# A sink as a 385th column of each head's logits, and inverses taken two heads at a time, in a hybrid encoder layer on one Trainium2 core

## The chip, the core and the metric

The kernel runs on one core of one Trainium2 chip. Five engines work side by side, each through its own list of instructions in a fixed order: TensorE (PE, with its weight loads as a list PEld of their own in the profile), VectorE (DVE), ScalarE (ACT), GpSimd (POOL) and SyncE (SP), which here issues most of the DMAs. An engine waits on a semaphore where its next instruction needs what another has made. The metric is the device time of one execution in microseconds (us); lower is better. Matmuls write to PSUM, everything else lives in SBUF with 128 partitions.

## What is computed

One encoder layer over 4096 tokens of 1024 numbers. Half of the mixing is attention within a window, with eight query heads on two key heads and a learned sink for each head; the other half is a pooling mixer. Both are gated, multiplied by an output matrix, normalised and added to the input.

```python
def banded_attention(q, k, v, rel_bias, sink):
    ...
    s = jnp.einsum('bnqkgd,bnskd->bnkgqs', qb, kw).astype(jnp.float32) * scale
    ...
    s = jnp.where(valid[None, :, None, None], s + bias[None, None], NEG)
    sk = sink.astype(jnp.float32).reshape(1, 1, N_KV_HEADS, Q_PER_KV, 1, 1)
    m = jnp.maximum(jnp.max(s, axis=-1, keepdims=True), sk)
    p = jnp.exp(s - m)
    p = p / (jnp.sum(p, axis=-1, keepdims=True) + jnp.exp(sk - m))
    o = jnp.einsum('bnkgqs,bnskd->bnqkgd', p.astype(v.dtype), vw)
    return o.reshape(B, S, N_Q_HEADS * HEAD_DIM)

def reference(x, pre_norm_g, w_in, rel_bias, attn_sink, pool_w, pool_scale, w_out, post_norm_g):
    ...
        h = rmsnorm(x, pre_norm_g[l])
        proj = jnp.einsum('bsd,de->bse', h, w_in[l])
        q, k, v, g_a, u_p, g_p = jnp.split(proj, splits, axis=-1)
        ...
        a = banded_attention(q, k, v, rel_bias, attn_sink[l]) * jax.nn.silu(g_a)
        p = multiscale_pool(u_p, pool_w[l], pool_scale[l]) * jax.nn.silu(g_p)
        mixed = jnp.einsum('bse,ed->bsd', jnp.concatenate([a, p], axis=-1), w_out[l])
        x = x + rmsnorm(mixed, post_norm_g[l])
    return x
```

A block of 128 queries sees three blocks of keys (its own and both neighbours), which makes 384 logits for each query and head; the first and the last block of the sequence see two, 256 logits. The sink has no key and no value: it only adds one term to the sum of exponentials, and takes part in the maximum.

## The kernel before, in words

The program has two phases. In the first, up to about 488 us, it normalises the input, scales the weights, and makes the gates and the pooling half. There the table of biases for the attention is made as well: `bias_load` fetches it into the tile `ybig` (the name `bias` is a view of it, eight heads by 384 columns, and `gpost` is another view behind it), `bias_head` (L679, on DVE) rescales and masks it head by head, and `bias_scales` makes `nsink`, the negative sinks (L658, DVE, 128x8).

In the second phase the 32 blocks are gone through from the last to the first (b = 31, 30, ... 0). Each block has two visits (half 0 and 1) with four of the eight heads each, so there are 64 visits. One visit, written (b, half), is this chain across the engines:

- `scores` (PE, L1530) puts the products of queries and keys into the two PSUM tiles of `s_bank`, two heads in each.
- `logits` (DVE, L1548), one custom instruction for each head: adds the bias, negates and scales, writes the result to the tile `p_all`, and leaves the smallest value, with the negative sink among the candidates, in `nm` (the negated maximum).
- `exps` (ACT, L1559), one for each head: exponentials in place in `p_all`, and their sum in `den`.
- `sinks` (DVE, L1566, 128x4): `nm` minus `nsink`, into `rd`; `sink_exps` (ACT, L1575, 128x4): its exponential, the sink's term.
- `denominators` (DVE): add the sink's term to `den` (L1579), take the reciprocal (L1580), multiply by a constant (L1581), all 128x4.
- `probs` (ACT, L1595), one for each head: `p_all` times the inverse, as float16, into `pn`. `rests` (DVE, L1603), one for each head: what float16 left out, as a second float16.
- `turn` (SP, L1615): one DMA that transposes `pn` into `pt_all`. Some time later, `values` (PE, L1849 and L1872) multiplies it by the values.

There is one `p_all` and one pair of `s_bank` tiles, and two buffers of `pn`. `logits` and `exps` go through the heads as i = 0 to 3 with `jj, gg = divmod(i, 2)` and `hh = 2 * gg + jj`, so the heads come in the order 0, 2, 1, 3; `probs` and `rests` go 0, 1, 2, 3.

Between the visits PE makes the projections of queries and keys (L1756, L1714, L1493), and the product with the output matrix (L2019) in several parts, for whose operands ACT, DVE and POOL make sums and casts (L1921 to L1963, tiles `y`, `ys`, `yf`, `at`), and whose partial results DVE adds up (L2061, tiles `mo` and `xt`).

The order on each engine is fixed by a plan. Every step is entered with a due time by `due(t, fn, ...)`; the list is sorted by these numbers, and instructions go out in that order whatever the engines do. `visit` sets the time t at which a visit's softmax starts, and `softmax` enters its steps at set distances from t. `settled` moves other steps (casts, sums, additions) away from the places that the softmax steps take, by rules on t alone. The last part of the program has its times written out, with `soft` in the place of `softmax`. So a step's place among its neighbours follows from these distances, and a step that leaves or joins at the same distance leaves the neighbours in place.

Of the kernel before, what the change touches and what calls it, by code (L numbers as in the profile page):

```python
# [8 lines left out]
F32 = mybir.dt.float32  # L9
# [20 lines left out]
QR = 32  # L30
NK = 2 * P + QR

W_BUFS = 6
# [38 lines left out]
def hybrid_layer(ctx: ExitStack, tc, io, out):  # L72
# [28 lines left out]
    wq_a = raw16[:, 4 * D :].rearrange("p (s a j k c) -> p s a j k c", s=4, a=2, j=2, k=HK)  # L101
    yflat = ybig.rearrange("p s d -> p (s d)")
    bias = yflat[:, : NH * 3 * P].rearrange("p (h k) -> p h k", h=NH)
    gpost = yflat[:, NH * 3 * P :]

# [49 lines left out]
    with ExitStack() as actx:  # L155
# [484 lines left out]
        def bias_load():  # L640

            f0 = f_scr[0:1, 0, :]
            for p0 in range(0, P, FR):
                nc.sync.dma_start(
                    bias[p0 : p0 + FR],
                    bass.AP(
                        tensor=f0.tensor, offset=f0.offset + P - 1 - p0,
                        ap=[[NF - 1, FR], [(FR + 1) * NF, NH], [1, 3 * P]],
                    ),
                )  # L650
# [27 lines left out]
        def bias_head(h):  # L678
            nc.vector.scalar_tensor_tensor(  # L679
                out=bias[:, h, :], in0=bias[:, h, :], scalar=invc[:, h : h + 1], in1=row_t["m"],  # L680
                op0=ALU.mult, op1=ALU.add,
            )
# [709 lines left out]
        for h in range(NH):  # L1392
            at_(7, 28.0 + 1.2 * h, bias_head, h)

        for m in range(1, NM):
# [158 lines left out]
    def exps(b, half, i):  # L1554
        nk = len(keys(b)) * P
        jj, gg = divmod(i, 2)
# [16 lines left out]
    def sink_exps(b, half):  # L1573
        es = rd_t[b, half][:, 1]
        nc.scalar.activation(es, es, AF.Exp)  # L1575

    def denominators(b, half):
        den, rd = den_t.pop((b, half)), rd_t[b, half]
        nc.vector.tensor_tensor(out=den, in0=den, in1=rd[:, 1], op=ALU.add)  # L1579
        nc.vector.reciprocal(rd[:, 0], den)  # L1580
        nc.vector.tensor_scalar(  # L1581
            out=rd[:, 0], in0=rd[:, 0], scalar1=P_SCALE, scalar2=None, op0=ALU.mult
        )
# [5 lines left out]
    def probs(b, half, i):  # L1589
        nk = len(keys(b)) * P  # L1590
        if i == 0:
            pn_t[b, half] = pb.tile(
# [24 lines left out]

    starts = []

    def softmax(b, half, t):  # L1620
# [707 lines left out]
    def soft(b, half, tl, te, td, tp, tr, tt):  # L2328

        at_(tl + 2.5, sinks, b, half)  # L2330
        at_(te + 2.6, sink_exps, b, half)
        for i in range(4):
            at_(tl + 0.62 * i, logits, b, half, i)
            at_(te + 0.65 * i, exps, b, half, i)
            at_(tp + 0.55 * i, probs, b, half, i)
            at_(tr + 0.62 * i, rests, b, half, i)
        at_(td, denominators, b, half)
# [189 lines left out]
```

## Time and profile before

| what | value |
|---|---|
| time, median of three runs | 1161.64 us |
| the three runs | 1160.58, 1161.64, 1161.92 us |
| the profiled execution's own time | 1160.95 us |
| its span (first to last instruction) | 1159.2 us |
| TensorE clock granted, mean | 0.998 of full speed |
| ACT busy | 757.9 us |
| POOL busy | 287.1 us |

In what follows, a row of the timeline reads: start in us, duration in us, engine, line of the kernel, operation, out<-in, shape, how many in a run (x), and in brackets how long the engine stood idle before it and what released it. A run of several rows of one kind is drawn together, with the time from the first start to the last end. A row of the groups reads: line, engine, operation, out<-in, shape, count, then the busy time in us and the mean duration of one in ns, then the idle time just before them. A row of windows reads: window, its length, busy us of PE, PEld, DVE, ACT and POOL (with the count of instructions), the granted clock, the share of DMA time and GB/s. A row with "SPq" is a DMA on the queue that SyncE issues, from issue to landing.

### The profile page before, as it was taken

How to read it: one execution, taken by the hardware profiler on the slowest of the kernel's cores; microseconds unless marked ns; L12 is line 12 of the kernel's file. 1: busy time of each engine (PE TensorE's matmuls, PEld its weight loads, DVE VectorE, ACT ScalarE, POOL GpSimd, SP SyncE). 2: the span in 40 equal slices, each digit the busy share in tenths (PEclk: the TensorE clock that was granted, in tenths of full speed). 3: DMA queues.
4: the chain of work that ended last, by engine and by line, in shares of the span. 5: the costliest groups of instructions: out<-in, count | busy, mean ns of one | idle time of the engine just before them, and what ended most of it. 6: DMA issues, size and time to landing. Idle time of an engine off the chain costs nothing.

```text
span 1159.2 us, 29335 instructions
## 1 busy us (share of the span) xinstructions
PE 1123.2 (97%) x11952; PEld 828.6 (71%) x11952; DVE 923.8 (80%) x1910; ACT 757.9 (65%) x1696; POOL 287.1 (25%) x273
## 2 busy tenths in 40 slices
PE   5999999999999999999899999999999999999997
PEld 4548888888888888887576676667666666766643
DVE  5888787788878976957887878878778778778896
ACT  5766666676465535156687767767777777777673
POOL 1000000000000000001364444445354454544322
PEclk9999999999999999999999999999999999999999
DMA  9567898796979856999799999899799899899977
GB/s 257 159 234 265 216 268 286 261 312 221 305 225 284 267 210 165 342 280 254 202 196 219 216 224 199 192 227 201 173 228 221 182 219 222 198 223 211 174 190 215
DMA packets 312630, 264.92 MB, mean 229 GB/s; under 512 B 214528, under 2 KB 275584, under 8 KB 303792
## 3 DMA queue, kind: packets, MB, share of 16 engines
q1 hardware_dynamic: 308464, 248.38, 77.8%
q0 software_dynamic: 4032, 14.68, 7.6%
q8 instruction: 93, 1.52, 0.5%
q14 instruction: 41, 0.34, 0.1%
HBM read 132.97 MB, written 79.21 MB: 183 GB/s over the span
## 4 chain that ended last, share of the span: by engine, by line
PE 61%; DVE 13%; DMA 11%; issue 5%; ACT 4%; SPq 1%; POOL 1%; DVEq 0%; POOLq 0%; ACTq 0%
PE ms L2019 12%; PE aq_p L1756 10%; PE m L2019 9%; PE ch L990 5%; PE s L1530 4%; DMA rs_scr<-ssq 3%; PE kv L1493 3%; PE kv L1714 3%; PE a L940 3%; PE cl L990 3%; DVE ws L855 3%; PE o L1872 3%; DMA xn<-in_x 2%; DVE xt L303 2%; DMA pt_all<-pn 2%
## 5 line engine op out<-in xcount | busy, mean ns | idle before, releaser
L990 PEld LDWEIGHTS <-wa 128*128 128x128 f16 x3360 | 328.8, 98 | 44.4 <-issue 6.6
L990 PE MATMUL ch<-xt,wa 128*128 128x256 f16 x1920 | 212.6, 273 | 2.7 <-ACT cbig L1002 2.6
L1559 ACT ACTIVATE p_all<-p_all,nm 128x384 f32<-128x384 f32 (+1 forms) x256 | 152.4, 596 | 41.5 <-DVE nm L1548 41.5
L1603 DVE SCALAR_TENSOR_TENSOR pn<-p_all,rd,pn 128x384 f16<-128x384 f32 (+1 forms) x256 | 144.4, 623 | 36.9 <-ACT pn L1595 36.2
L2019 PE MATMUL ms<-wo,ys 128*128 128x512 f16 x720 | 165.4, 379 | 3.8 <-DVE xt L2061 1.3
L1595 ACT ACTIVATE pn<-p_all,rd 128x384 f16<-128x384 f32 (+1 forms) x256 | 134.7, 597 | 36.7 <-DVE rd L1581 17.6
L1548 DVE CUSTOM_DVE_ANT_0 p_all<-s,ybig,nsink 128x384 f32<-128x384 f32 (+1 forms) x256 | 155.7, 664 | 1.7 <-PE s L1530 1.7
L2019 PEld LDWEIGHTS <-ys 128*128 128x128 f16 x720 | 68.8, 98 | 85.2 <-issue 4.1
L2019 PE MATMUL m<-wo,y 128*128 128x512 f16 x540 | 124.0, 379 | 1.4 <-DVE mo L2061 1.3
L990 PE MATMUL cl<-xt,wa 128*128 128x256 f16 x960 | 106.9, 273 | 2.5 <-DVE u L1015 1.4
L1925 POOL TENSOR_TENSOR y<-yf,y 128x512 f16<-128x512 f32 x29 | 33.6, 1159 | 268.2 <-DMA wo<-w_scr 158.7
L2019 PEld LDWEIGHTS <-y 128*128 128x128 f16 x540 | 51.6, 98 | 62.4 <-issue 2.8
L1756 PEld LDWEIGHTS <-raw 128*128 128x128 f16 x864 | 83.2, 98 | 17.6 <-issue 5.7
L211 POOL TENSOR_SCALAR ssq<-ssq 128x4 f32<-128x4 f32 (+1 forms) x11 | 4.8, 440 | 346.7 <-ACT jk L202 340.8
L1756 PE MATMUL aq_p<-xt,raw 128*128 128x256 f16 x672 | 77.9, 273 | 0.0
L303 DVE TENSOR_TENSOR xt<-ybig,xt 128x1024 f16<-128x1024 f32 x56 | 67.2, 1218 | 13.1 <-ACT xt L298 13.1
L1925 POOL TENSOR_TENSOR ys<-at,ys 128x512 f16<-128x512 f32 x28 | 33.8, 1206 | 147.1 <-ACT ys L1921 123.5
L1024 ACT ACTIVATE gp<-cbig,cg 128x256 f32<-128x256 f32 x42 | 19.0, 499 | 69.7 <-DVE cbig L1015 66.5
L2056 POOL TENSOR_TENSOR mo<-mo,ybig 128x512 f32<-128x512 f32 x39 | 51.3, 1316 | 41.8 <-ACT jkb L2045 41.6
L1530 PE MATMUL s<-k_all,q 64*32 64x288 f16 (+2 forms) x2856 | 60.1, 284 | 1.5 <-ACT k_all L1481 0.9
L298 ACT CAST xt<-ybig 128x1024 f16<-128x1024 f32 x56 | 57.1, 1040 | 4.0 <-PE cl L990 2.1
L1756 PE MATMUL aq_p<-xt,wq_b 128*128 128x256 f16 x504 | 58.6, 273 | 0.0
(212 smaller groups left out, 1947.5 us busy)
## 6 DMA issues: line engine op xcount, KB each, us to landing
x_scr<-xt SPq DMA_DIRECT2D x16, 1024.0 KB, 4.0
xt<-x_scr SPq DMA_DIRECT2D x16, 1024.0 KB, 5.0
xn<-in_x SPq DMA_DIRECT2D x28, 512.0 KB, 7.2
ybig<-in_xT SPq DMA_DIRECT2D x28, 512.0 KB, 6.9
y_scr<-xt SPq DMA_DIRECT2D x14, 1024.0 KB, 8.6
xt<-y_scr SPq DMA_DIRECT2D x14, 1024.0 KB, 6.2
mo<-in_x POOLq DMA_DIRECT2D x28, 512.0 KB, 7.2
out<-mo SPq DMA_DIRECT2D x28, 512.0 KB, 7.0
```

The source lines that it names most:

```text
L298: nc.scalar.copy(couple(m, c)[:, w, 0], y_view(i))
L303: eng.tensor_tensor(out=o[:, w, 1], in0=y_view(i), in1=o[:, w, 0], op=ALU.subtract)
L990: nc.tensor.matmul(acc[:, c], wa[:, q, wi, slot * HK + k, c * P : (c + 1) * P], x[:, xi, k, :], start=(fresh and n == 0), stop=(n > 3 * 2 ...
L1530: nc.tensor.matmul(s_bank[jj][r0 : r0 + nr, gg, lo:hi], q_t[u, half][a, qi, jj, tl + r0 : tl + r0 + nr], k_all[a, ki, k0 : k0 + hi - lo], ...
L1548: nc.vector.tensor_tensor_reduce(out=p_t[b, half][:, hh, :nk], in0=s_t[b, half][jj][:, gg, :nk], in1=bias[:, h, lo : lo + nk], scale=negc[ ...
L1559: nc.scalar.activation(p[:, hh, :nk], p[:, hh, :nk], AF.Exp, bias=nm_t[b, half][:, hh : hh + 1], scale=-1.0, accum_out=den_t[b, half][:, h ...
L1595: nc.scalar.activation(prob_view(b, half)[:, 0, i], p_t[b, half][:, i, :nk], AF.Copy, scale=rd_t[b, half][:, 0, i : i + 1],)
L1603: nc.vector.scalar_tensor_tensor(out=pn4[:, 1, i], in0=p_t[b, half][:, i, :nk], scalar=rd_t[b, half][:, 0, i : i + 1], in1=pn4[:, 0, i], o ...
L1756: nc.tensor.matmul(acc[:, jj], w[:, wi, jj, k, :], x[:, xi, k, :], start=(first and n == 0), stop=(last and n > 3 * 2 * HK - 3), skip_grou ...
L1925: eng.tensor_tensor(out=y[:, :, 1], in0=f(u), in1=y[:, :, 0], op=ALU.subtract)
L2019: nc.tensor.matmul(z_t[u, tag], y[:, k, yi, :], wo[o][:, wi, k, :], start=(n == 0 and acc is None), stop=(n == 3 * HK - 1), skip_group_che ...
L2056: eng.tensor_tensor(out=mo, in0=mo, in1=gpost[:, cs], op=ALU.mult)
```

## The change

For the 30 blocks that are not at an end of the sequence (`inner(b)`, 60 of the 64 visits) the sink becomes one more column of the logits. A row of the bias is now 386 wide (`BW`), of which 385 (`NC`) are used; column 384 holds the sink times `invc` (made once by `bias_sinks`, a 128x8 multiplication on DVE), and column 384 of the PSUM tiles is set to zero once (`zero_column`, two memsets on DVE of 128x2). `logits` and `exps` run over 385 columns, so that the sum of exponentials has the sink's term in it; `probs`, `rests` and `turn` still take 384. In these visits `sinks`, `sink_exps` and the addition L1579 are gone. The reciprocal and the multiplication are done twice, over two heads each (128x2): by `inverses(b, half, 0)` for heads 0 and 2 at the distance at which `sinks` stood, and by `inverses(b, half, 1)` for heads 1 and 3 at that of `denominators`. `probs` and `rests` take the heads in the order 0, 2, 1, 3. The four visits of the blocks 31 and 0 keep the steps of before. In the written-out last part, `soft` is changed as `softmax` is.

```diff
+NC = 3 * P + 1
+BW = 3 * P + 2
...
-    ybig = const.tile([P, 4, D], F32, name="ybig")
+    yflat = const.tile([P, NH * BW + D], F32, name="ybig")
+    ybig = yflat[:, : 4 * D].rearrange("p (s d) -> p s d", s=4)
...
-    bias = yflat[:, : NH * 3 * P].rearrange("p (h k) -> p h k", h=NH)
-    gpost = yflat[:, NH * 3 * P :]
+    bias = yflat[:, : NH * BW].rearrange("p (h k) -> p h k", h=NH)
+    gpost = yflat[:, NH * BW :]
...
         def bias_head(h):
             nc.vector.scalar_tensor_tensor(
-                out=bias[:, h, :], in0=bias[:, h, :], scalar=invc[:, h : h + 1], in1=row_t["m"],
-                op0=ALU.mult, op1=ALU.add,
+                out=bias[:, h, : 3 * P], in0=bias[:, h, : 3 * P], scalar=invc[:, h : h + 1],
+                in1=row_t["m"], op0=ALU.mult, op1=ALU.add,
+            )
+
+        def bias_sinks():
+
+            def column(t):
+                return t.rearrange("p (h o) -> p h o", o=1)
+
+            nc.vector.tensor_tensor(
+                out=bias[:, :, 3 * P : NC], in0=column(row_t["sk"]), in1=column(invc), op=ALU.mult
+            )
...
+        at_(7, 37.0, bias_sinks)
...
-    p_all = pb1.tile([P, 4, 3 * P], F32, name="p_all")
+    p_all = pb1.tile([P, 4, BW], F32, name="p_all")
...
+    def inner(b):
+        return 0 < b < NB - 1
+
+    def columns(b):
+        return NC if inner(b) else len(keys(b)) * P
+
+    def zero_column():
+        for i in range(2):
+            nc.vector.memset(s_bank[i][:, :, 3 * P : NC], 0.0)
+
+    due(0.0, zero_column)
...
     def logits(b, half, i):
-        kbs = keys(b)
-        nk, lo, j0 = len(kbs) * P, kbs[0] * P, 2 * half
+        nk, lo, j0 = columns(b), keys(b)[0] * P, 2 * half
...
     def exps(b, half, i):
-        nk = len(keys(b)) * P
+        nk = columns(b)
...
+    def inverses(b, half, j):
+        den, rd = den_t[b, half][:, j : 4 : 2], rd_t[b, half][:, 0, j : 4 : 2]
+        nc.vector.reciprocal(rd, den)
+        nc.vector.tensor_scalar(out=rd, in0=rd, scalar1=P_SCALE, scalar2=None, op0=ALU.mult)
+
     def denominators(b, half):
+        if inner(b):
+            return inverses(b, half, 1)
...
     def softmax(b, half, t):
         starts.append(t)
-        due(t + 2.8, sinks, b, half)
-        due(t + 3.25, sink_exps, b, half)
+        if inner(b):
+            due(t + 2.8, inverses, b, half, 0)
+        else:
+            due(t + 2.8, sinks, b, half)
+            due(t + 3.25, sink_exps, b, half)
         for i in range(4):
             due(t + 0.1 + 0.67 * i, logits, b, half, i)
             due(t + 0.8 + 0.8 * i, exps, b, half, i)
-            due(t + 4.5 + 0.6 * i, probs, b, half, i)
-            due(t + 5.1 + 0.62 * i, rests, b, half, i)
+            due(t + 4.5 + 0.6 * i, probs, b, half, ORDER[i])
+            due(t + 5.1 + 0.62 * i, rests, b, half, ORDER[i])
         due(t + 4.3, denominators, b, half)
         due(t + 7.8, turn, b, half)
```

In the program as it is built, the lists of PE, POOL and SP are the same before and after, waits included. ACT's list is 60 rows shorter, by the 60 `sink_exps`. DVE's is 3 rows longer, by the two memsets and the product of `bias_sinks`; in each of the 60 visits four small instructions stand where four stood.

On ACT, the visit (30, 0), the first of the inner ones. A name such as `pn_0_6416` is a tile, its buffer and a running number; "x4" is four instructions of one kind in a row. Before:

```order
L1559 ACTIVATE p_all,den_0_6400<-p_all,nm_0_6399 128x384 x4
L1575 ACTIVATE rd_0_6401<-rd_0_6401 128x4
L1595 ACTIVATE pn_0_6416<-p_all,rd_0_6401 128x384 x4
L1921 CAST y_15_6449<-yf_15_6011 128x4x128
L1481 ACTIVATE q_0_6451<-aq_0_6347 128x512
```

and after the change (the line numbers are those of the changed kernel):

```order
L1582 ACTIVATE p_all,den_0_6403<-p_all,nm_0_6402 128x385 x4
L1625 ACTIVATE pn_0_6418<-p_all,rd_0_6404 128x384 x4
L1955 CAST y_15_6451<-yf_15_6014 128x4x128
L1493 ACTIVATE q_0_6453<-aq_0_6350 128x512
```

The exponentials of the four heads are now followed directly by `probs`.

On DVE, the visit (28, 0), with two steps of other work among its own: `kq` belongs to a projection, `mo` is a partial sum of the output product. Before:

```order
L1566 TENSOR_TENSOR rd_0_6994<-nm_0_6992,nsink 128x4
L1806 SCALAR_TENSOR_TENSOR kq_1_7019<-aq_p_6958,kq_1_6216 128x512
L1579 TENSOR_TENSOR den_0_6993<-den_0_6993,rd_0_6994 128x4
L1580 RECIPROCAL rd_0_6994<-den_0_6993 128x4
L1581 TENSOR_SCALAR rd_0_6994<-rd_0_6994 128x4
L1603 SCALAR_TENSOR_TENSOR pn_0_7065<-p_all,rd_0_6994,pn_0_7065 128x384 x3
```

and after:

```order
L1602 RECIPROCAL rd_0_6993<-den_0_6992 128x2
L1603 TENSOR_SCALAR rd_0_6993<-rd_0_6993 128x2
L1840 SCALAR_TENSOR_TENSOR kq_1_7019<-aq_p_6957,kq_1_6219 128x512
L1602 RECIPROCAL rd_0_6993<-den_0_6992 128x2
L1603 TENSOR_SCALAR rd_0_6993<-rd_0_6993 128x2
L1633 SCALAR_TENSOR_TENSOR pn_0_7063<-p_all,rd_0_6993,pn_0_7063 128x384 x3
```

One reciprocal and one multiplication now stand ahead of the other work, in the place of `sinks`, and one of each behind it, in the place of three instructions.

On DVE, the visit (27, 0), where an addition of the output product (`mo`) stands right behind the step that changes. Before:

```order
L1566 TENSOR_TENSOR rd_0_7293<-nm_0_7291,nsink 128x4
L2061 TENSOR_TENSOR mo_1_7221<-ms_15_7278,mo_1_7221 128x512
L1579 TENSOR_TENSOR den_0_7292<-den_0_7292,rd_0_7293 128x4
L1580 RECIPROCAL rd_0_7293<-den_0_7292 128x4
L1581 TENSOR_SCALAR rd_0_7293<-rd_0_7293 128x4
```

and after:

```order
L1602 RECIPROCAL rd_0_7290<-den_0_7289 128x2
L1603 TENSOR_SCALAR rd_0_7290<-rd_0_7290 128x2
L2095 TENSOR_TENSOR mo_1_7218<-ms_15_7275,mo_1_7218 128x512
L1602 RECIPROCAL rd_0_7290<-den_0_7289 128x2
L1603 TENSOR_SCALAR rd_0_7290<-rd_0_7290 128x2
```

The addition has two instructions ahead of it where it had one.

More of the change, by code (lines that the diff above doesn't have):

```diff
@@ L644, in bias_load @@
                 nc.sync.dma_start(
-                    bias[p0 : p0 + FR],
+                    bias[p0 : p0 + FR, :, : 3 * P],
                     bass.AP(
@@ L2328, in soft @@
     def soft(b, half, tl, te, td, tp, tr, tt):
-        at_(tl + 2.5, sinks, b, half)
-        at_(te + 2.6, sink_exps, b, half)
+        if inner(b):
+            at_(tl + 2.5, inverses, b, half, 0)
+        else:
+            at_(tl + 2.5, sinks, b, half)
+            at_(te + 2.6, sink_exps, b, half)
         for i in range(4):
@@ L2334, in soft @@
             at_(te + 0.65 * i, exps, b, half, i)
-            at_(tp + 0.55 * i, probs, b, half, i)
-            at_(tr + 0.62 * i, rests, b, half, i)
+            at_(tp + 0.55 * i, probs, b, half, ORDER[i])
+            at_(tr + 0.62 * i, rests, b, half, ORDER[i])
         at_(td, denominators, b, half)
```

4 lines of the change are left out of this document (2 added, 2 removed).

## The prediction

> **What bounds the kernel now.** I read the page's first part, then the windows of the second phase, then the timeline of PE for every place where it waits.
>
> ```profile
> PE 1123.2 (97%) x11952; PEld 828.6 (71%) x11952; DVE 923.8 (80%) x1910; ACT 757.9 (65%) x1696; POOL 287.1 (25%) x273
> ...
> 900.00:1000.00 100.00, 100.00 (x1265) 66.71 (x1263) 78.63 (x206) 74.57 (x187) 45.89 (x43) 1.00 0.89 202
> ```
>
> PE is busy for 97% of the span, and in the hundred microseconds from 900 for all of it, at full clock. A softmax that gets shorter there is worth nothing: DVE's 78.63 and ACT's 74.57 lie under PE's work. The change touches nothing on PE, so what it can win is the idle time of PE. Behind 488 us the waits of PE above 0.2 us are these:
>
> ```profile
> 488.16 0.71 PE L1756 MATMUL aq<-xt,raw 128*128 128x256 f16 x5 [0.21 <-DVE u L1015]
> ...
> PE s L1530 <- ACT k_all L1481: 0.9, 2, 0.5
> ...
> 525.28 1.91 PE L1756 MATMUL aq<-xt,raw 128*128 128x256 f16 x16 [1.14 <-DVE q L1484]
> ...
> 554.65 0.60 PE L2019 MATMUL ms<-wo,ys 128*128 128x512 f16 x2 [0.53 <-ACT ys L1921]
> ...
> 555.89 2.33 PE L2019 MATMUL ms<-wo,ys 128*128 128x512 f16 x10 [0.63 <-POOL ys L1925]
> ...
> 573.92 2.75 PE L2019 MATMUL m<-wo,y 128*128 128x512 f16 x12 [1.30 <-DVE mo L2061]
> ...
> 577.12 2.75 PE L2019 MATMUL ms<-wo,ys 128*128 128x512 f16 x12 [0.44 <-DVE mo L2061]
> ...
> 622.98 0.85 PE L1849 MATMUL o<-pt_all,vv 128*64 128x256 f16 x12 [0.90 <-DMA pt_all<-pn]
> ...
> 769.28 1.92 PE L1493 MATMUL kv<-xt,raw 128*128 128x256 f16 x16 [1.13 <-DVE den L1579]
> ...
> 805.90 0.85 PE L1849 MATMUL o<-pt_all,vv 128*64 128x256 f16 x12 [0.35 <-DMA pt_all<-pn]
> ...
> 1115.34 4.92 PE L2019 MATMUL ms<-wo,ys 128*128 128x512 f16 x22 [0.85 <-DVE ys L1925]
> ...
> 1121.22 0.50 PE L1530 MATMUL s<-k_all,q 64*128 64x256 f16 x6 [0.42 <-DVE nm L1548]
> ...
> 1122.02 2.75 PE L2019 MATMUL ms<-wo,ys 128*128 128x512 f16 x12 [0.29 <-DVE xt L2061]
> ...
> 1127.88 2.32 PE L2019 MATMUL ms<-wo,ys 128*128 128x512 f16 x10 [1.03 <-DVE xt L2061]
> ```
>
> They sum to 10.1 us: 9.22 in the thirteen rows with a start, 0.9 in the two waits of the scores for `k_all`. Those two lie in the visits of block 31, which the change leaves alone, and the 0.21 stands ahead of the first visit. At most some 9 us, 0.8% of the time, can be had, in a start-up (525 to 577), three single places, and the last blocks (1115 to 1128).
>
> **The cost of the wider rows.**
>
> ```profile
> L1548 DVE CUSTOM_DVE_ANT_0 p_all<-s,ybig,nsink 128x384 f32<-128x384 f32 x240 | 147.9, 672 | 0.0
> ...
> L855 DVE TENSOR_TENSOR ws<-ws 128x521 f32<-128x521 f32 x16 | 11.2, 703 | 0.6
> ...
> L1548 DVE CUSTOM_DVE_ANT_0 p_all<-s,ybig,nsink 128x256 f32<-128x256 f32 x16 | 7.7, 540 | 1.7 <-PE s L1530 1.7
> ```
>
> A custom instruction of 384 columns takes 672 ns and one of 256 takes 540, so a column costs (672-540)/128 = 1.0 ns, and the 385th 4 ns a visit. That an odd count is dearer no row of the custom instruction can show; the nearest row with an odd count is 521 columns at 703 ns, against 0.69 us for 512 in the row of L1484 below, the same 1 ns a column. I take 0 for both `logits` and `exps`. The other end: 60 ns an instruction, 0.24 us a visit, as much as a quarter of what a visit gains below.
>
> **The three new instructions ahead.**
>
> ```profile
> 464.73 0.62 DVE L679 SCALAR_TENSOR_TENSOR ybig<-ybig,invc,mask 128x384 f32<-128x384 f32 x1 [4.90 <-DMA ybig<-f_scr]
> ...
> 464.73:488.16 23.43, 22.68 (x208) 20.02 (x206) 22.74 (x38) 4.21 (x11) 0.00 (x0) 1.00 0.96 358
> ```
>
> The memsets come on DVE shortly before the 4.90 us that it waits for the bias: covered, 0; without that cover they would cost 0.3, two at the price of the smallest instructions shown below. `bias_sinks` stands behind the wait, in a stretch where DVE is busy for 22.74 of 23.43 us up to the row at 488.16, at which PE waits for DVE. It costs its length there: **+0.2** (0.16 for a small one, a little for the stride of 386); from 0 to 0.5.
>
> **One visit.** The first inner visit, (30, 0):
>
> ```profile
> 519.89 0.60 ACT L1559 ACTIVATE p_all<-p_all,nm 128x384 f32<-128x384 f32 x1
> 520.49 0.19 ACT L1575 ACTIVATE rd<-rd 128x4 f32<-128x4 f32 x1
> ...
> 520.91 0.18 DVE L1580 RECIPROCAL rd<-den 128x4 f32<-128x4 f32 x1
> 521.12 0.17 DVE L1581 TENSOR_SCALAR rd<-rd 128x4 f32<-128x4 f32 x1
> 521.38 2.13 ACT L1595 ACTIVATE pn<-p_all,rd 128x384 f16<-128x384 f32 x4 [0.70 <-ACT rd L1575]
> ...
> 522.02 2.21 DVE L1603 SCALAR_TENSOR_TENSOR pn<-p_all,rd,pn 128x384 f16<-128x384 f32 x4 [0.73 <-ACT pn L1595]
> ...
> 524.54 0.69 DVE L1484 SCALAR_TENSOR_TENSOR q<-aq,q 128x512 f16<-128x512 f32 x1 [0.31 <-ACT q L1481]
> ```
>
> The exponentials end at 520.49; the sink's exponential and three small instructions on DVE follow, and the first of `probs` starts at 521.38. After the change the inverses of heads 0 and 2 are made while the last two exponentials run, so `probs` can start at 520.5: 0.88 us sooner. The second pair needs one reciprocal and one multiplication behind the last exponential, done at about 521.0, and the third of `probs` would come at 520.5 + 2 x 0.53 (2.13 for four) = 521.56, so it waits for nothing. `rests` (0.64 behind), the copy of q on ACT, and the addition at 524.54 move with it. PE's 1.14 at 525.28 falls to about 0.3: **-0.86**, from 0 to -1.14.
>
> Where ACT has other work between the exponentials and `probs`, less is won:
>
> ```profile
> 548.81 0.19 ACT L1575 ACTIVATE rd<-rd 128x4 f32<-128x4 f32 x1
> 548.90 0.57 ACT L2045 ACTIVATE jkb<-m 128x512 bf16<-128x512 f32 x1
> 549.69 2.13 ACT L1595 ACTIVATE pn<-p_all,rd 128x384 f16<-128x384 f32 x4
> ```
>
> Here, in (29, 1), the square `jkb` starts 0.09 sooner and its end, not the inverse, releases `probs`: 549.69 - 548.90 = 0.79 is left from its start to the first of `probs`, of which 0.57 remains, so 0.09 + 0.22 = 0.3. The other visit of block 29 I put at 0.4, also with a filler. DVE's chain to the sums that PE waits for at 554.65 and 555.89 is that much earlier: **-0.73** of the 1.16 there, from 0 to -1.16.
>
> The 1.30 at 573.92 hangs on `mo`, which in DVE's order stands behind the `rests` of both visits of block 28. Each gains 0.6 to 0.8, by the same reckoning, together more than the stall: **-1.30**, from 0.
>
> At 577.12 it goes the other way. In the third order of the section on the change, `mo` has two dependent small instructions ahead of it where it had one that it could follow at once.
>
> ```profile
> 576.30 0.16 DVE L1566 TENSOR_TENSOR rd<-nm,nsink 128x4 f32<-128x4 f32 x1
> 576.38 0.68 DVE L2061 TENSOR_TENSOR mo<-ms,mo 128x512 f32<-128x512 f32 x1
> ```
>
> It started 0.08 after `sinks`; dependent small instructions follow each other at 0.21 (520.91 to 521.12), so two of them take 0.41: **+0.33**, from 0.1 to 0.8.
>
> **The transposes.** PE's 0.90 at 622.98 waits for a transpose:
>
> ```profile
> 596.82 0.63 DVE L1566 TENSOR_TENSOR rd<-nm,nsink 128x4 f32<-128x4 f32 x1
> ...
> 601.53 7.68 SPq L1615 DMA_TRANSPOSE pt_all<-pn  x1
> ```
>
> The transposes come one behind another, this one taking 7.68 us. I let half a microsecond of the visit's gain through: **-0.5**, from 0 to -0.9. The 0.35 at 805.90 is of the same kind: **-0.3**. At 769.28 the addition of `den` is named, but PE's matmul reads the loaded `xt`, not `den`; I leave the 1.13 as it is: 0, from -1.13.
>
> **The end.**
>
> ```profile
> 1095.00:1128.00 33.00, 30.29 (x294) 15.50 (x293) 30.13 (x71) 22.95 (x61) 6.30 (x5) 1.00 0.74 189
> ...
> 1116.46 2.13 ACT L1595 ACTIVATE pn<-p_all,rd 128x384 f16<-128x384 f32 x4 [1.61 <-issue]
> ```
>
> DVE is busy for 30.13 of 33 us and paces PE: waits of 0.85, 0.42, 0.29 and 1.03. Its list has as many small instructions in an inner visit as before; what goes is its own wait for ACT (0.73 ahead of `rests`, as at 522.02), in the two visits of block 1. In the second of these ACT had been free for 1.61 us ahead of 1116.46, so `probs` can be done before DVE comes, and 0.8 is won; of the first I count nothing more, since its gain is met by PE's own pace: **-0.8**, from 0 to -2.6.
>
> **The sum.** +0.2 - 0.86 - 0.73 - 1.30 + 0.33 - 0.5 - 0.3 - 0.8 = -3.96. The profiled execution took 1160.95, so 1156.99; the median of the runs shown is 0.69 above it, and 1157.7 is the time to compare.
>
> **A rule against the change.** The multiplication has moved to a place where POOL is often at work.
>
> ```profile
> 558.36 1.16 POOL L1925 TENSOR_TENSOR ys<-at,ys 128x512 f16<-128x512 f32 x1
> 558.56 0.98 DVE L1581 TENSOR_SCALAR rd<-rd 128x4 f32<-128x4 f32 x1
> ...
> L1566 DVE TENSOR_TENSOR rd<-nm,nsink 128x4 f32<-128x4 f32 x64 | 21.1, 329 | 2.2
> ```
>
> A TENSOR_SCALAR of 0.17 took 0.98 and ended with POOL's instruction, and `sinks`, at 0.16 when alone, took 0.329 on the mean, so its place often meets one. The Trainium skill ("SBUF — State Buffer", "Who interferes with whom") says that the port pair which DVE and GpSimd share is an exclusive lock: whoever issues first has it for the whole instruction, and the other stands still. The row at 558.56 agrees with it; by that rule each of the 60 first multiplications could stand still for a whole POOL instruction. The price goes by the rows: 0.98 - 0.17 = 0.81 a meeting. But two exponentials pass between the first multiplication's place and the end of the visit's exponentials, 1.2 us at the 0.60 of the row at 519.89, and a POOL instruction of 1.16 ends within that. I count nothing.
>
> **The rivals.**
>
> The transposes pin the stream (chance 0.16). If the DMA queue, not the softmax, sets when the transposes ahead of 622.98 land, the 3 us won before it are lost as a longer wait there, and only 805.90 and the end are left: -1.1, so **1160.5**. For it: 7.68 us for one transpose, and DMA 0.89 to 0.96 busy in the two windows above. Against it: a transpose is issued when `rests` end, and these come sooner.
>
> It does little (0.08). DVE issues no fewer small instructions in a visit than before; only their places differ. If the copies and squares on ACT cover the gap in most of the places above, as `jkb` half does, and the multiplications take the rest, it is under 0.5: **1161.3**.
>
> Slower (0.07): the lock above. It decides where POOL's instructions come in pairs, so that the first multiplication outlasts the 1.2 us, and where DVE sets the pace: the two visits each of the start-up's and the end's blocks. At five such places with 0.81 each and nothing won it is +4: **1165.7**. `sinks` stood in the same place under the same lock, which speaks against any loss over before.
>
> More goes (0.09): all the waits that a softmax feeds vanish, 7.44 of the 9.22 without those at 488.16, 577.12 and 769.28; with +0.2 and +0.33 that is -6.9: **1154.7**.
>
> **How the numbers follow.** The forecast has 0.60, from 1155.8 to 1159.3: the bounds of its terms add up to 3.4 us below the sum (without the 1.13 at 769.28) and 5.3 above it, and as the terms don't all err together I give it 1.9 below and 1.6 above. 0.2% of the median is 2.3 us, about what a measurement of this kernel can tell from no change; faster by more than that is 0.60 + 0.09 = 0.69, the same 0.16 + 0.08 = 0.24, slower 0.07. A range to 1161.2 takes in the forecast, most of the pinned case and part of the one that does little; down to 1155.0 it takes a part of the best one; some 2 in 10 are left out.
>
> **What would show it.** In the profile after: `probs` right behind the exponentials at (30, 0), 0.9 sooner against `scores`; DVE's wait for ACT ahead of `rests` (0.73) gone where ACT has a filler; PE's waits at 525, 554, 556 and 574 together under 1 us, the one at 577 near 0.8; the first custom instructions of 385 columns at 0.67 us. A longer wait at 622.98 would show the transposes; `rests` starting as late as before would show a cover that I missed; custom instructions or exponentials clearly above their 0.67 and 0.60 would make the whole forecast wrong, since 240 of each then add to DVE and ACT.

## The result, and the profile after

The changed kernel takes 1161.44 us (median of 20 runs, 1157.72 to 1163.02), the kernel before 1163.71 (median of 20, 1160.17 to 1166.80): a ratio of 0.9977 with a 95% interval of 0.9966 to 0.9988, or 1.4 to 4.0 us less. The forecast was faster by 4.0 us, 1157.7, with a range to 1161.2; the time lies 0.2 us above it. Two things are in this miss. The kernel before took 1161.64 in the three runs that the forecast started from, and 2.1 more in twenty; and of the 4.0 us only 2.3 came by the two medians, or 2.7 by the ratio (1163.71 x 0.0023).

The page's first part, of the profiled execution after the change:

```profile
PE 1123.0 (97%) x11952; PEld 828.7 (72%) x11952; DVE 923.5 (80%) x1913; ACT 748.5 (65%) x1636; POOL 295.4 (25%) x273
```

ACT, without the 60 sink exponentials, is busy for 9.4 us less, and DVE's busy time is what it was. POOL has the same 273 instructions as before, but is busy for 295.4 us instead of 287.1: some of its instructions take longer, and rows further down show one that waits inside. The groups of the changed lines (columns as in the section on the profile before), and behind them that of `rests` in the kernel before:

```profile
L1571 DVE CUSTOM_DVE_ANT_0 p_all<-s,ybig,nsink 128x385 f32<-128x385 f32 x240 | 148.2, 676 | 0.0
...
L1633 DVE SCALAR_TENSOR_TENSOR pn<-p_all,rd,pn 128x384 f16<-128x384 f32 x240 | 145.0, 664 | 18.0 <-ACT pn L1625 17.3
...
L1603 DVE TENSOR_SCALAR rd<-rd 128x2 f32<-128x2 f32 x120 | 31.4, 262 | 4.1
...
L1602 DVE RECIPROCAL rd<-den 128x2 f32<-128x2 f32 x120 | 19.4, 162 | 5.5 <-ACT p_all L1582 5.1
```

```profile
L1603 DVE SCALAR_TENSOR_TENSOR pn<-p_all,rd,pn 128x384 f16<-128x384 f32 x240 | 137.1, 630 | 35.0 <-ACT pn L1595 34.2
```

The 385th column costs 4 ns of 676, its odd number included. What DVE no longer spends waiting for `probs` ahead of the first `rests` (18.0 us now, 35.0 before) it partly spends inside `rests`, 664 ns each instead of 630.

The visit (30, 0) in the timeline, to be set against the one of before:

```profile
522.35 0.60 ACT L1582 ACTIVATE p_all<-p_all,nm 128x385 f32<-128x385 f32 x1
522.35 0.17 DVE L1603 TENSOR_SCALAR rd<-rd 128x2 f32<-128x2 f32 x1
522.95 2.12 ACT L1625 ACTIVATE pn<-p_all,rd 128x384 f16<-128x384 f32 x4
523.07 0.17 DVE L1602 RECIPROCAL rd<-den 128x2 f32<-128x2 f32 x1 [0.55 <-ACT p_all L1582]
...
523.58 2.21 DVE L1633 SCALAR_TENSOR_TENSOR pn<-p_all,rd,pn 128x384 f16<-128x384 f32 x4
```

The last exponential ends at 522.95 and the first of `probs` starts there; it was 0.89 behind. The mechanism works as meant. PE's waits behind the first phase (those above 0.4 us, without the two of block 31):

```profile
526.05 0.52 PE L1906 MATMUL o<-pt_all,vv 128*64 128x256 f16 x6 [1.19 <-DMA pt_all<-pn]
...
558.00 0.39 PE L2053 MATMUL ms<-wo,ys 128*128 128x512 f16 x1 [0.63 <-POOL ys L1959]
...
803.98 0.30 PE L1883 MATMUL o<-pt_all,vv 128*64 128x256 f16 x2 [0.66 <-DMA pt_all<-pn]
...
1048.43 0.41 PE L1883 MATMUL o<-pt_all,vv 128*64 128x256 f16 x4 [1.80 <-DMA pt_all<-pn]
...
1114.77 0.39 PE L2053 MATMUL ms<-wo,ys 128*128 128x512 f16 x1 [0.65 <-DVE ys L1959]
...
1120.18 0.38 PE L1554 MATMUL s<-k_all,q 64*128 64x256 f16 x3 [0.49 <-DVE nm L1571]
...
1121.11 0.29 PE L1554 MATMUL s<-k_all,q 64*128 64x256 f16 x2 [0.42 <-DVE nm L1571]
...
1127.77 0.38 PE L2053 MATMUL ms<-wo,ys 128*128 128x512 f16 x1 [1.03 <-DVE xt L2095]
```

The waits at 525, 574 and 577 are gone, the one at 554 is small. In their place stand waits for transposes, above all 1.80 at 1048, where before there was none; and the end still has waits much like those of before.

To find the place, take the start of the same matmul in every run. The table gives the first matmul of the second phase (488.16 in the prediction's rows) from the span's start, and behind it, counted from there, the matmuls that started at 525.28, 573.92, 622.98, 769.28, 1048.54 and 1115.34 before, and the span's end. The runs below the third row belong to the next section.

| run | first phase | 525 | 574 | 623 | 769 | 1048 | 1115 | end |
|---|---|---|---|---|---|---|---|---|
| before | 488.16 | 37.13 | 85.77 | 134.83 | 281.12 | 560.39 | 627.18 | 671.0 |
| before, again (r_before) | 487.06 | 37.13 | 85.78 | 135.27 | 280.42 | 559.50 | 626.30 | 670.1 |
| after | 490.60 | 37.31 | 83.97 | 131.43 | 276.46 | 557.83 | 624.17 | 668.4 |
| after, again (r_after) | 487.44 | 36.24 | 82.90 | 130.56 | 278.17 | 559.21 | 625.55 | 669.9 |
| after, third (r_after2) | 484.69 | 37.04 | 83.71 | 131.62 | 276.62 | 558.06 | 624.40 | 668.7 |
| tables only (e_layout) | 487.71 | 37.13 | 85.79 | 134.77 | 280.35 | 559.28 | 626.09 | 669.9 |
| column alone (e_late) | 488.11 | 36.87 | 83.67 | 131.47 | 277.48 | 556.25 | 622.45 | 666.1 |
| after, copies in (5, 1) (e_pause) | 486.24 | 36.88 | 83.55 | 131.54 | 277.52 | 556.78 | 623.11 | 667.4 |
| the same, (1, 1) not split (e_p11) | 484.86 | 36.24 | 82.90 | 131.16 | 276.23 | 556.06 | 622.13 | 665.7 |
| split at the start only (e_start) | 485.31 | 37.22 | 83.90 | 131.58 | 278.55 | 559.89 | 626.10 | 669.7 |
| the same, copies in six visits (e_start2) | 485.49 | 36.83 | 83.51 | 130.89 | 276.81 | 557.13 | 623.60 | 667.2 |
| after, copies in six, (1, 1) not split (e_robust) | 487.66 | 36.24 | 82.90 | 130.96 | 276.85 | 556.47 | 622.54 | 666.1 |

Down to 769 the change wins 2 to 5 us in its three executions. From 769 to 1048 it needs 281.0 to 281.4 where the kernel before needs 279.1 to 279.3: 2 us are given back in a stretch where PE had hardly waited at all. And from 1115 to the end 0.4 is lost (43.8 to 43.9 before, 44.3 after).

### The profile page after: what moved, and what is told of

Read it like the earlier page. It is cut to its first block, busy times and chain, and to the rows that moved or that the text cites. A ratio compares the mean times of both kernels' runs of the same rounds, so it can differ in the third digit from the quotient of the medians.

```text
span 1159.0 us, 29568 instructions
## 1 busy us (share of the span) xinstructions
PE 1123.0 (97%) x11952; PEld 828.7 (72%) x11952; DVE 923.5 (80%) x1913; ACT 748.5 (65%) x1636; POOL 295.4 (25%) x273
## 3 DMA queue, kind: packets, MB, share of 16 engines
q8 instruction: 93, 1.52, 0.5%
## 4 chain that ended last, share of the span: by engine, by line
PE 63%; DVE 12%; DMA 9%; issue 6%; ACT 2%; SPq 1%; POOL 0%; DVEq 0%; POOLq 0%; ACTq 0%
PE ms L2053 12%; PE aq_p L1790 10%; PE m L2053 9%; PE ch L1001 6%; PE s L1554 4%; PE cl L1001 4%; PE a L951 3%; PE kv L1748 3%; PE kv L1505 3%; PE o L1906 3%; DVE ws L866 3%; DMA rs_scr<-ssq 2%; DVE xt L305 2%; DMA pt_all<-pn 2%; DMA xn<-in_x 1%
## 5 line engine op out<-in xcount | busy, mean ns | idle before, releaser
L1582 ACT ACTIVATE p_all<-p_all,nm 128x385 f32<-128x385 f32 (+1 forms) x256 | 152.9, 599 | 46.6 <-DVE nm L1571 45.8
L1633 DVE SCALAR_TENSOR_TENSOR pn<-p_all,rd,pn 128x384 f16<-128x384 f32 (+1 forms) x256 | 152.3, 655 | 20.0 <-ACT pn L1625 19.3
L1571 DVE CUSTOM_DVE_ANT_0 p_all<-s,ybig,nsink 128x385 f32<-128x385 f32 (+1 forms) x256 | 155.9, 667 | 1.7 <-PE s L1554 1.7
L2090 POOL TENSOR_TENSOR mo<-mo,ybig 128x512 f32<-128x512 f32 x39 | 54.7, 1402 | 44.7 <-ACT jkb L2079 44.7
```

Of the source, the lines that this page charges most:

```text
L1571: nc.vector.tensor_tensor_reduce(out=p_t[b, half][:, hh, :nk], in0=s_t[b, half][jj][:, gg, :nk], in1=bias[:, h, lo : lo + nk], scale=negc[ ...
L1582: nc.scalar.activation(p[:, hh, :nk], p[:, hh, :nk], AF.Exp, bias=nm_t[b, half][:, hh : hh + 1], scale=-1.0, accum_out=den_t[b, half][:, h ...
L1633: nc.vector.scalar_tensor_tensor(out=pn4[:, 1, i], in0=p_t[b, half][:, i, :nk], scalar=rd_t[b, half][:, 0, i : i + 1], in1=pn4[:, 0, i], o ...
L2090: eng.tensor_tensor(out=mo, in0=mo, in1=gpost[:, cs], op=ALU.mult)
```

## The experiments

The theory (A): the gain is real, and part of it is given back where ACT, which is now ahead, sends a cast to POOL so much sooner that POOL's instruction starts just before one of DVE's `rests` and locks it out. The rivals: the wider tables cost the first phase 2.4 us (B); the transposes wait for the busy DMA queues (C); the end is bound by DVE's count of instructions (D).

**Both kernels again.** No edit.

> The kernel before, unchanged, a second profile. Theory A (what the first phase lacks or has more is scatter from one execution to the next, and the change only acts behind it): the first matmul of the second phase's projection, at 488.2 us in the first profile, may come anywhere from 486 to 491, and from there to the span's end it is 671.0 +- 0.5 us. Theory B (the wider bias rows cost the first phase 2.4 us): the first phase ends at 488.2 +- 0.4.

> The changed kernel, unchanged, a second profile and more times. Theory A: the first phase ends anywhere from 486 to 491; the second phase takes 666.5 us where the rests of visit (5, 1) end before POOL's cast starts, 668.4 where POOL comes first and the transpose behind it is late as in the first profile. Theory B: the first phase ends at 490.6 +- 0.4 again. Either way the time is 1 to 4.5 us under the kernel before.

> The changed kernel a third time, beside the two below on one chip. Theory A (a lock that is always there, not chance): the last of the rests of (5, 1) takes 1.5 us again and that of (1, 1) too, PE waits 1.5 us or more for the transpose at 1046 to 1049, and the time is 0.997 to 0.999 of the kernel before, clearly above the next run.

The first phase of the kernel before took 487.06 in its second profile, that of the changed kernel 487.44 and 484.69 after 490.60. It scatters by 6 us with the change in, below what I had allowed too, and theory B falls already here. The second phase of the kernel before took 670.1, a little under the expected 670.5: the wait at 769 (1.13 in the first profile) didn't come. The changed kernel's 669.9 is above the 668.4 of the first profile, with that wait (1.0) and one of 1.4 for a transpose at 638 in it. As to times, the changed kernel stands at 0.9975 (0.9962 to 0.9988) of the kernel before in one series and 0.9986 (0.9977 to 0.9995) in the other.

PE's wait at 1048 came in all three profiles. In the second and the third:

```profile
1046.65 0.85 PE L1883 MATMUL o<-pt_all,vv 128*64 128x256 f16 x12 [1.75 <-DMA pt_all<-pn]
```

```profile
1042.75 0.85 PE L1883 MATMUL o<-pt_all,vv 128*64 128x256 f16 x12 [1.80 <-DMA pt_all<-pn]
```

So it isn't chance. The transpose it waits for is that of visit (5, 1). Its `rests`, POOL and the queue in the first profile after (the third row is the last of the four `rests` alone):

```profile
1036.13 3.11 DVE L1633 SCALAR_TENSOR_TENSOR pn<-p_all,rd,pn 128x384 f16<-128x384 f32 x4
1037.63 1.19 POOL L1959 TENSOR_TENSOR ys<-at,ys 128x512 f16<-128x512 f32 x1 [3.85 <-ACT ys L1955]
1037.71 1.52 DVE L1633 SCALAR_TENSOR_TENSOR pn<-p_all,rd,pn 128x384 f16<-128x384 f32 x1
...
1039.30 3.64 SPq L1645 DMA_TRANSPOSE pt_all<-pn  x1
```

and the same place in the kernel before:

```profile
1038.09 2.20 DVE L1603 SCALAR_TENSOR_TENSOR pn<-p_all,rd,pn 128x384 f16<-128x384 f32 x4
1039.94 1.38 POOL L1925 TENSOR_TENSOR ys<-at,ys 128x512 f16<-128x512 f32 x1 [4.25 <-ACT ys L1921]
1040.36 3.71 SPq L1615 DMA_TRANSPOSE pt_all<-pn  x1
```

The last of the four `rests`, 0.61 alone, took 1.52, since POOL had started 0.08 us earlier; the four took 3.11 instead of 2.20. Before, the POOL instruction started at 1039.94, behind the start of the last of `rests`, and was the one that waited. In the visits of the same kind after the change, (9, 1) for one, DVE is first by 0.03 us:

```profile
956.50 0.61 DVE L1633 SCALAR_TENSOR_TENSOR pn<-p_all,rd,pn 128x384 f16<-128x384 f32 x1
956.53 1.60 POOL L1959 TENSOR_TENSOR ys<-at,ys 128x512 f16<-128x512 f32 x1 [3.85 <-ACT ys L1955]
```

and POOL stands still, 1.60 instead of 1.19; PE has no wait behind it. At (5, 1) DVE's steps, from an addition (`mo`, L2084) on, come 0.10 us later behind ACT's `probs` than at its sisters, and that decides it. That a DVE instruction with two inputs in SBUF and a GpSimd instruction that reads SBUF shut each other out for a whole instruction, by which came first, is what the Trainium skill says ("SBUF — State Buffer", "Who interferes with whom"); these two pairs of rows show both orders.

An SPq row, against what the section on the profile before says, doesn't last until the landing: its duration is the time in which SyncE issues the DMA. By the view of the tile `pt_all` the transpose of (5, 1), 3.64 us in its row, landed 9.1 us behind its issue, and the one of before, 3.71 in its row, 7.0 us. Before, it was there 1.2 us ahead of PE's matmul at 1048.54. After, counted from the matmul at 769, it is issued 1.2 us later and lands 3.2 us later. The later issue alone would have about used up that lead, and no more; the wait comes from the longer landing.

One thing goes along with the longer landing. POOL, which came first, is also sooner at its next steps, among them the issue of a load of 512 KB into `mo`. After, and then before:

```profile
1040.31 0.90 POOL L2124 DMA_DIRECT2D mo<-in_x  x1
```

```profile
1042.49 0.88 POOL L2090 DMA_DIRECT2D mo<-in_x  x1
```

It is issued 1.0 us behind the transpose after, and 2.1 before. In the four profiles of all runs in which `rests` are locked out at a visit of this kind ((5, 1) in three, (9, 1) in one further down) the load comes 1.0 us behind the issue and the transpose lands in 9.0 to 9.3 us; at the same two visits without the lock the load comes 2.1 to 2.2 behind, and the transpose lands in 6.9 to 7.9, where the profile tells it. That the load makes the landing longer isn't shown, since no run moved it alone. And the lock by itself need not cost anything: it also comes at (20, 0), in all three profiles after (1.56 to 1.57 for the last of `rests`), but PE uses that transpose 19 us behind its issue, and doesn't wait.

**The tables alone.** Logits, exponentials, sinks and denominators as before, on 384 columns; the wide rows, the sink's column and the zero column are made and not used.

```diff
     def columns(b):
-        return NC if inner(b) else len(keys(b)) * P
+        return len(keys(b)) * P
...
-        if inner(b):
-            due(t + 2.8, inverses, b, half, 0)
-        else:
-            due(t + 2.8, sinks, b, half)
-            due(t + 3.25, sink_exps, b, half)
+        due(t + 2.8, sinks, b, half)
+        due(t + 3.25, sink_exps, b, half)
...
-    ORDER = (0, 2, 1, 3)
+    ORDER = (0, 1, 2, 3)
```

> Only the tables of the change: rows of 386, the sink's column and the zero column are made, but logits, exponentials, sinks and denominators work as before on 384 columns. Theory A: second phase 671.0 +- 0.7, time within 1 us of the kernel before. Theory B: first phase at 490.6, time 2.4 us above the kernel before.

First phase 487.71, second 669.9 (0.4 below the range expected, and beside 671.0 and 670.1 of the kernel before itself), time 0.9998 (0.9986 to 1.0010) of the kernel before. The tables cost nothing that can be seen; theory B is out.

**The column alone.** All four heads' inverses at once, behind the exponentials.

```diff
-    def inverses(b, half, j):
-        den, rd = den_t[b, half][:, j : 4 : 2], rd_t[b, half][:, 0, j : 4 : 2]
+    def inverses(b, half):
+        den, rd = den_t[b, half], rd_t[b, half][:, 0]
...
-        if inner(b):
-            due(t + 2.8, inverses, b, half, 0)
-        else:
+        if not inner(b):
             due(t + 2.8, sinks, b, half)
...
-    ORDER = (0, 2, 1, 3)
+    ORDER = (0, 1, 2, 3)
```

> The column alone: 385 columns, no sinks, no sink exponential, no addition, but the reciprocal and the multiplication of all four heads in one, at the place of the denominators, heads in the order 0 to 3. If the removed steps on the chain are the gain, the first of the probabilities at (30, 0) starts 0.45 us behind the exponentials (0.88 before, 0.00 with the change), as early as with the change wherever ACT has a filler of 0.57 us, and the second phase takes 667.5 to 669, some two thirds of the whole gain. If the split in two is the gain, it is 0.8 behind and the second phase takes 670.5 to 671.

```profile
519.86 0.60 ACT L1582 ACTIVATE p_all<-p_all,nm 128x385 f32<-128x385 f32 x1
520.58 0.18 DVE L1602 RECIPROCAL rd<-den 128x4 f32<-128x4 f32 x1 [0.84 <-ACT p_all L1582]
520.80 0.17 DVE L1603 TENSOR_SCALAR rd<-rd 128x4 f32<-128x4 f32 x1
521.05 2.13 ACT L1625 ACTIVATE pn<-p_all,rd 128x384 f16<-128x384 f32 x4 [0.50 <-ACT p_all L1582]
```

`probs` follow the exponentials by 0.59 here, a third of the way (0.45 was expected). Yet the second phase takes 666.1, less than was expected and less than with the whole change, and the time is 0.9970 (0.9957 to 0.9983). By 623 it has won what the whole change has won (131.47 against 130.56 to 131.62), and from 769 to 1048 it loses nothing (278.8): no lock at (5, 1), where POOL comes 0.06 us behind the last of `rests`, and none at (1, 1). The split adds little to the gain of the column, and in these profiles the loss comes with it; but 0.06 us is a narrow escape, and a run further down shows the loss without the split at its place.

**POOL pushed away at one place.** Three small copies on ACT in visit (5, 1), which nothing reads, in the changed kernel.

```diff
             scale=rd_t[b, half][:, 0, i : i + 1],
         )
+        if (b, half, i) == (5, 1, 3):
+            for _ in range(3):
+                nc.scalar.activation(rd_t[b, half][:, 1], nm_t[b, half], AF.Copy)
```

> The changed kernel with three small copies (128x4) added on ACT in visit (5, 1), behind the four probabilities, and nothing else. They push ACT's next cast, and with it POOL's instruction, by some 0.27 us. Theory A (two executions of the changed kernel lost 1.0 us in the rests of (5, 1) since POOL's cast starts 0.08 us ahead of the last of them and locks it out, and PE waits 1.9 us at 1046 to 1048 for the transpose that is late by this): the four rests of (5, 1) take 2.2 us instead of 3.1, PE's wait for the transpose behind it falls from 1.9 to under 0.5, and the second phase is 1.5 to 1.9 shorter than it would be: 666.5 to 668. Rival C (the transpose is late by the DMA queues, which are busy there anyway): PE's wait stays at 1.5 or more.

```profile
1032.34 0.66 ACT L1631 ACTIVATE rd<-nm 128x4 f32<-128x4 f32 x3
1032.56 2.20 DVE L1636 SCALAR_TENSOR_TENSOR pn<-p_all,rd,pn 128x384 f16<-128x384 f32 x4
1034.63 1.16 POOL L1962 TENSOR_TENSOR ys<-at,ys 128x512 f16<-128x512 f32 x1 [4.42 <-ACT ys L1958]
1034.82 3.65 SPq L1648 DMA_TRANSPOSE pt_all<-pn  x1
```

The `rests` take 2.20 again, POOL starts 0.5 behind the last of them, and PE's matmul on the transpose starts without a wait:

```profile
1043.02 0.85 PE L1886 MATMUL o<-pt_all,vv 128*64 128x256 f16 x12
```

From 769 to 1048 it is 279.3, 1.8 to 2.2 less than in the changed kernel, though three instructions were added, and the time is 0.9954 (0.9939 to 0.9969). This settles for (5, 1) that the meeting of POOL and `rests` starts the loss. It doesn't rule out rival C for the rest of the way: the copies also put the load of `mo` back to 2.1 us behind the transpose, which lands in 7.2 us again.

**The last visit not split.** As above, and (1, 1) takes the four inverses at once.

```diff
+    def split(b, half):
+        return inner(b) and (b, half) != (1, 1)
...
     def inverses(b, half, j):
-        den, rd = den_t[b, half][:, j : 4 : 2], rd_t[b, half][:, 0, j : 4 : 2]
+        w = slice(j, 4, 2) if split(b, half) else slice(0, 4)
+        den, rd = den_t[b, half][:, w], rd_t[b, half][:, 0, w]
...
-        if inner(b):
+        if split(b, half):
             at_(tl + 2.5, inverses, b, half, 0)
-        else:
+        elif not inner(b):
```

> As the run before it, and visit (1, 1) takes all four inverses at the place of the denominators, as the column alone did. Theory A: the rests of (1, 1) take 2.2 us instead of 3.1, and from the product at 1095 to the last matmul it is 56.6 us instead of 57.4, as with the column alone. Rival D (the end is bound by its number of instructions on DVE): 57.2 to 57.4 as in every other run.

In the changed kernel (1, 1) has the lock as well:

```profile
1115.69 1.12 ACT L1625 ACTIVATE pn<-p_all,rd 128x384 f16<-128x384 f32 x2 [0.40 <-DVE rd L1603]
1116.11 3.10 DVE L1633 SCALAR_TENSOR_TENSOR pn<-p_all,rd,pn 128x384 f16<-128x384 f32 x4
1117.40 1.38 POOL L1959 TENSOR_TENSOR ys<-s,ys 128x512 f16<-128x512 f32 x1 [3.23 <-ACT ys L1955]
```

and with the late inverses it hasn't:

```profile
1108.56 2.21 DVE L1640 SCALAR_TENSOR_TENSOR pn<-p_all,rd,pn 128x384 f16<-128x384 f32 x4
1110.63 1.16 POOL L1966 TENSOR_TENSOR ys<-s,ys 128x512 f16<-128x512 f32 x1 [4.24 <-ACT ys L1962]
```

From 1095 (607.00 behind the phase's start before, 604.44 after, 602.67 here) to the last matmul (664.35, 661.80, 659.12) it is 57.35 before, 57.36 after and 56.45 here. The end wins 0.9. This run also has two small instructions less on DVE in (1, 1), as rival D would want it, but they aren't what wins: counted from the same matmul at 1095, the four `rests` start at 21.95 before, 21.07 after and 21.03 here, and end at 24.15, 24.17 and 23.24. What the change wins ahead of them it loses inside them, and here it doesn't. From that matmul to the last one the five runs without the lock at (1, 1), the column alone and those still to come among them, win 0.5 to 0.9 on the kernel before; the three profiles of the changed kernel and the run with copies in (5, 1) alone, all with the lock, win nothing.

**The split at the start only.** `split` is `26 <= b < NB - 1`, in the changed kernel without copies.

> The inverses in two pairs only in blocks 30 to 26, where PE waits for the softmax; in blocks 25 to 1 all four at the place of the denominators. Theory A: the start of the second phase as with the change (PE's product at 574 comes 82.9 us behind the phase's start, the one at 594 at 102.8, where the column alone had 83.7 and 103.9), the rest as with the column alone (no lock at (5, 1), none at (1, 1)): second phase 664.7 to 666, time 0.995 to 0.997 of the kernel before, the fastest of all. Rival C: what is won by 594 is lost again in longer waits for transposes, and the second phase takes 667 or more.

This missed: 669.7, where 664.7 to 666 was expected (its time was 0.9964, 0.9949 to 0.9979). Part of it is waits that come and go (1.1 at 763, 1.1 at 520). But 2 us are a lock again, at another visit, (9, 1):

```profile
951.88 3.11 DVE L1637 SCALAR_TENSOR_TENSOR pn<-p_all,rd,pn 128x384 f16<-128x384 f32 x4
953.41 1.16 POOL L1963 TENSOR_TENSOR ys<-at,ys 128x512 f16<-128x512 f32 x1 [4.16 <-ACT ys L1959]
...
955.05 3.68 SPq L1649 DMA_TRANSPOSE pt_all<-pn  x1
...
964.35 0.85 PE L1887 MATMUL o<-pt_all,vv 128*64 128x256 f16 x12 [1.73 <-DMA pt_all<-pn]
```

There the 0.1 us delay of DVE came at (9, 1) and not at (5, 1). So it is the hair's breadth between POOL and the last of `rests`, not the split, that has to go; with late inverses it is 0.06 us instead of 0.03.

**POOL pushed away in all visits of the kind.** The copies in (25, 1), (21, 1), (17, 1), (13, 1), (9, 1) and (5, 1): in the kernel split at the start only, and in the changed kernel with (1, 1) not split.

```diff
-        if (b, half, i) == (5, 1, 3):
+        if b % 4 == 1 and b > 1 and (half, i) == (1, 3):
```

> The split in blocks 30 to 26 alone, as run before, with the three copies in the same six visits. In that run the lock had come at (9, 1), where an addition of DVE started 0.12 us later than at its sisters, and PE waited 1.9 us at 962. Theory A: with POOL's cast moved away from the rests that wait is gone (under 0.5), and the second phase is 1.5 to 2 us shorter than the 669.7 of then, 667 to 668.2 (less where the wait for the loaded xt at 763, 1.2 then, doesn't come). Rival C: a wait of over 1.5 us for a transpose between 940 and 1050 again.

> The changed kernel with the three small copies on ACT in all six visits of the kind of (5, 1) (blocks 25, 21, 17, 13, 9 and 5, half 1), and all four inverses at the place of the denominators in (1, 1). Theory A: no lock at these visits, POOL's cast some 0.4 us behind the last of the rests; second phase 665 to 667, time 0.994 to 0.997 of the kernel before and 1.5 to 3.5 us under the changed kernel on the same chip. Rival C (transposes wait for the DMA queues): no better than the changed kernel.

The first takes 667.2 instead of 669.7 and has no wait of over 1 us for a transpose between 940 and 1050; its time is 0.9957 (0.9944 to 0.9970). The second has the lock nowhere among the six; at (9, 1) POOL now starts 0.59 behind the last of `rests`, which starts 1.59 behind the first:

```profile
952.44 2.20 DVE L1640 SCALAR_TENSOR_TENSOR pn<-p_all,rd,pn 128x384 f16<-128x384 f32 x4
954.62 1.16 POOL L1966 TENSOR_TENSOR ys<-at,ys 128x512 f16<-128x512 f32 x1 [4.42 <-ACT ys L1962]
```

It takes 1153.52 us beside 1156.68 of the changed kernel and 1158.61 of the kernel before, on one chip: 0.9956 (0.9943 to 0.9970), against 0.9986 (0.9977 to 0.9995) for the changed kernel there. It beats both. Waits for other transposes remain in every run, up to 1.0 us in those with copies, 1.4 in the changed kernel, and at places that differ from run to run (638, 717, 798, 882); they aren't settled, and rival C may hold for them.

## Why the prediction was right or wrong

- **The bound, and one visit** (-0.86 at 525): right. In the second profile after, 36.24 behind the phase's start against 37.13, -0.89. In the other two a wait for the transpose of (31, 1) took all or nearly all of it away (37.31, 37.04): a wait in place of the one removed, that I hadn't priced there.
- **554 and 556** (-0.73): too large. The product at 554 started 66.49 behind the phase's start before and 65.09 in the second profile after, 0.5 sooner beyond the 0.89 above, and the 0.63 at 556 stayed. **574** (-1.30) gave a little more: from 554 to 574 it took 19.28 before and 17.81 after, 1.47 less. Together 1.98, where the terms sum to 2.03.
- **577** (+0.33): wrong in sign. The wait went. I let DVE's two instructions lie ahead of `mo` at their full length, and as if PE came as early as before relative to DVE. But this `mo` starts 3.27 behind the `mo` ahead of it after and 3.20 before, 0.07 more; and with the stall at 574 gone PE comes 0.5 later relative to DVE.
- **The transposes** (-0.5 at 623, -0.3 at 806): the first came, and more (from 577 to 623 it takes 44.7 to 45.2 instead of 45.9 and 46.3); the second didn't (0.35 became 0.66 in the first profile after). The row shown for the first was misread twice: 601.53 is the transpose of (26, 0), for which PE doesn't wait, and its 7.68 is the time of the issue. PE waited for that of (26, 1), issued at 611.80. The rival of the pinned transposes leaned on the same 7.68. The 1.13 at **769** was one execution's: absent in the second profile of the same kernel.
- **The end** (-0.8): right in size where there is no lock (-0.9 in the run with copies and (1, 1) not split), wrong for the change as it is (0.0). The first profile's 1.61 us of ACT ahead of `probs` was read as pure gain; it also let ACT send its cast 1.7 us sooner to POOL (counted from the matmul at 1095), whose instruction then started 0.29 us ahead of the last of `rests`.
- **The rule against the change**: this is the step that failed. I weighed the lock at the place that the diff moves, the first multiplication, and wrote "I count nothing". The multiplications do meet POOL, 262 ns on the mean of the 120 instead of 0.17 us, and no run shows a cost of it: the last run above, with the split in all inner visits but one, and the column alone, without it, both take 666.1 in the second phase. But I didn't ask what ACT, finishing sooner, sets off on POOL, and what of DVE it then meets; the sum has terms for waits that PE had, and none for a wait that it might get. That cost about 2 us behind (5, 1) and 0.9 at (1, 1), 2.9 of the 4.0 that were forecast. What starts it is shown; why the transpose of (5, 1) then takes 2 us longer to land stays open.
- **The wide rows** (0): right, 676 and 672 ns. **The added instructions of the first phase** (+0.2): lost in its scatter of 6 us, which may also be what moved the median that the forecast was set against.
- Without the two locks that cost time, the forecast's 4.0 would have held: 0.9956, of the last run above, is 5.1 us under the kernel before, with an interval of 3.5 to 6.6. That the sum comes so near is in part luck, since its terms err both ways (577 and 623 gave more than forecast, 554 and 806 less). And that the time missed the range by only 0.2 us says little, as the time that the forecast started from was itself 2.1 off.

## What to carry to other kernels

A step that makes an engine finish sooner is to be followed past the wait that it removes: what does that engine issue next, on which engine does that start work, and what does it meet there. Where two engines shut each other out, look for pairs whose starts lie within 0.1 us, since such a pair decides differently from visit to visit; a small delay on the engine that isn't the bound can be worth 2 us on the one that is, where the result is used soon: PE waited for a transpose that it uses 8 to 9 us behind the issue, and not for one that it uses 19 us behind. And where the profile shows a median of three, the base itself may be off by as much as the gain.

## What the runs showed of the hardware that was not expected

One addition of DVE, released by ACT, starts 0.10 to 0.12 us later in one visit than at its sisters, at the same visit in every profile of a kernel ((5, 1) in three of three of the changed one) and at another in a kernel with other code ((9, 1) in the one split at the start only). What causes it was not found. And the transpose of (5, 1), issued 1.2 us later, was 1.8 us late for PE: its landing took 9.1 us from the issue, where it took 7.0 in the kernel before. The load that POOL issued sooner behind it comes along with that in every such profile, and isn't shown to be the cause.
